# Layer norms with VectorE's order written by hand, ScalarE for the first tile's transposed copies, and a first product in the order of its operands

## The chip, the cores and the metric

The kernel runs on one core of a Trainium2 chip. The metric is the time of one execution on the device in microseconds (us), the median of several. The core's engines that matter here are TensorE (PE in the profile; its weight loads are PEld), VectorE (DVE), ScalarE (ACT), GpSimd (POOL) and SyncE (SP), which issues the transfers by DMA. Each engine works through its own list of instructions in a fixed order and waits, at an instruction, for what this instruction needs.

## What is computed

Two transformer blocks in a row, in fp32, on 256 tokens of width 1024. Block 1 has one layer: a state-space and Fourier mixer, and 32 experts of which each token uses four. Block 2 has two layers. Each has a mixer of four kinds of heads with an output projection, a layer norm over residual plus mixer, a feed-forward part (dense in the first layer, 8 experts of which two are used in the second), and another layer norm. Cut to what matters:

```python
def _layer_norm(x, g, b):
    mu = jnp.mean(x, -1, keepdims=True)
    var = jnp.mean(jnp.square(x - mu), -1, keepdims=True)
    return (x - mu) * lax.rsqrt(var + LN_EPS) * g + b

def second_block(x, ...):
    h = x.astype(F32)
    for l in range(DEPTH_2):
        p = jnp.einsum('btd,dc->btc', h, w_in[l])
        pa, pb, pc, pd = _split(p, MIXER_COLS)
        ...
        mix = jnp.einsum('btc,cd->btd', jnp.concatenate([ya, yb, yc, yd], axis=-1), w_out[l])
        h = _layer_norm(DN_ALPHA * h + mix, ln1_g[l], ln1_b[l])
        if l % 2 == 0:
            f = _swiglu(h, ffn_w_gate[i], ffn_w_up[i], ffn_w_down[i])
        else:
            f = _moe(h, moe_router[i], moe_w_gate[i], moe_w_up[i], moe_w_down[i])
        h = _layer_norm(DN_ALPHA * h + f, ln2_g[l], ln2_b[l])
    return h
```

## The kernel before

The tokens lie in two tiles of 128 partitions; `K.xres` holds the residual, [128, tile, 1024]. A phase ends with a product that TensorE accumulates in PSUM. A norm follows on VectorE, and `to_hT` transposes the normalised tiles (four 128x128 blocks to one PSUM tile, two such q per token tile) into `K.hT`, [128, 8, 256], with the features on the partitions: the operand of the next phase's products. Between `to_hT` and a product stands one more step: fp32 products are made of three products in fp32r, hi x hi, hi x lo and lo x hi (`mm3`, L340 to 344). `split` (L330) makes the two halves of weights: ScalarE copies the high half `whi` (L335), VectorE subtracts it, which is the low half `wlo` (L336). The activations are halved in the same way, one of eight blocks `kt` at a time (L1574 and L1575 in the mixers, L2204 and L2205 in the dense phase, L2165 and L2166 for the output projection, where the trace calls both halves w).

The phases of block 2 come in this order: mixer 0, norm (0,0), dense phase with 11 steps, norm (0,1), mixer 1, norm (1,0), expert phase with its router. The places between them are called seams here.

Each layer norm is done in two pieces. `layer_norm` (L1387) scales the residual and adds the product (L1403), takes the statistics (L1404, L1407), makes the reciprocal root in ten small steps (`rsqrt`, L233 to 245) and normalises (L1409). `to_hT` applies the weight and the bias of the norm to the transposed copy. The residual gets them later, in the next phase: `affine` (L1424) multiplies by a row and adds a row, each 128x1024 and for each token tile. These rows `lnr` come by DMA, spread over the partitions (`brow`, L313), and `affine_rows` issues them when the next phase runs. The residual that mixer 0 receives has one row to apply (the final norm's weight of block 1), so its affine is two instructions; that of mixer 1 is four. With `raw` (norm (1,0)) the transposed copies are made of the values before the normalisation.

The end of both mixers (L2166 to L2177) is the output projection. It goes over two halves of the features, half 1 first and half 0 last. Half 0 holds the outputs oH and oG of the two gated mixers, of which oG is last. Each half has two column halves c, whose sums for the two token tiles lie in PSUM, called pp (c = 0) and tr (c = 1), so that each (half, c) has 24 products. The rows `lnr` are queued on SyncE behind weight loads (`ahead("xb", 3)`), and the affine of the residual is written down with half 1.

The order on each engine is fixed when the kernel is built: a scheduler goes through the program by estimated times, and takes what is ready by them. `behind(K, ins)` places what stands in it after the instructions ins in that order. The order thus obtained holds on the chip, whatever the waits there are.

Of the kernel before, what the change touches and what calls it, by code (L numbers as in the profile page):

```python
# [8 lines left out]
F32 = mybir.dt.float32  # L9
BF = mybir.dt.bfloat16  # L10
I32 = mybir.dt.int32
F32R = mybir.dt.float32r
U8 = mybir.dt.uint8
AF = mybir.ActivationFunctionType
OP = mybir.AluOpType
# [209 lines left out]
def rsqrt(K, dst, src, scale, eps, iters=3):  # L225
# [10 lines left out]
    if n < 3:  # L236
        w = v
        nc.vector.tensor_scalar(w, src, -0.5 * scale, -0.5 * eps, op0=OP.mult, op1=OP.add)
        for k in range(iters):
            for c in range(n):  # L240
                c_ = slice(c, c + 1)
                nc.vector.tensor_scalar(t[:, c_], y[:, c_], w[:, c_], y[:, c_], op0=OP.mult, op1=OP.mult)
            for c in range(n):
                c_ = slice(c, c + 1)
                nc.vector.tensor_scalar((dst if k == iters - 1 else y)[:, c_], t[:, c_], 1.5, y[:, c_], op0=OP.add, op1=OP.mult)
        return
# [93 lines left out]
def mm3(K, ps, l, r, start, stop):  # L340

    K.nc.tensor.matmul(ps, lhsT=l[0], rhs=r[0], start=start, stop=False)  # L342
    K.nc.tensor.matmul(ps, lhsT=l[0], rhs=r[1], start=False, stop=False)  # L343
    K.nc.tensor.matmul(ps, lhsT=l[1], rhs=r[0], start=False, stop=stop)  # L344

# [1041 lines left out]
def layer_norm(K, A, ps, i, parts, alpha, hT, raw=False):  # L1387
# [10 lines left out]
    for tt in range(2):  # L1398
        x = h[:, tt, :]
        st = K.small.tile([128, 2, 6], F32, name="ln_s")  # L1400
        for c in range(2):
            xc = x[:, 512 * c:512 * c + 512]
            nc.vector.scalar_tensor_tensor(xc, xc, alpha, parts(tt, c), op0=OP.mult, op1=OP.add)  # L1403
            nc.vector.bn_stats(st[:, c, :], xc)  # L1404
        if raw:
            to_hT(K, ps, hT, tt, x, None)
        nc.vector.bn_aggr(mv[:, tt, :], st)  # L1407
        rsqrt(K, rs[:, tt:tt + 1], mv[:, tt, 1:2], 1.0, 1e-5)
        K.normed = nc.vector.tensor_scalar(x, x, mv[:, tt, 0:1], rs[:, tt:tt + 1], op0=OP.subtract, op1=OP.mult)  # L1409
        if not raw:  # L1410
            to_hT(K, ps, hT, tt, x, *K.lnc)
# [8 lines left out]
def affine(K, rows, tt):  # L1420

    x = K.xres[:, tt, :]
    for r_, op in zip(rows, (OP.mult, OP.add)):
        K.nc.vector.tensor_tensor(x, x, r_, op=op)  # L1424


def to_hT(K, ps, hT, tt, x, g, b=None):

    nc = K.nc
    for q in range(2):  # L1430
        pt = ps("tr", [128, 4, 128])
        transpose4(K, pt, [x[:, 128 * (4 * q + j):128 * (4 * q + j) + 128] for j in range(4)])
        if g is None:
            d = hT[:, 4 * q:4 * q + 4, 128 * tt:128 * tt + 128]
            if q:
                last = nc.scalar.activation(d, pt, AF.Copy)
            else:
                nc.vector.tensor_copy(d, pt)
            continue
        for j in range(4):  # L1440
            kt = 4 * q + j
            d = hT[:, kt, 128 * tt:128 * tt + 128]
            if b is None:
                if q:
# [3 lines left out]
            elif q:  # L1448
# [51 lines left out]
def mixers(K, A, l, nxt):  # L1500
# [71 lines left out]
    early = [split(K, w2, w0[0][:, :, 0:128], [128, 8, 128], bufs=2, after=(K.normed,))]  # L1572
    for kt in range(8):
        nc.scalar.activation(hT[0][:, kt, :], K.hT[:, kt, :], AF.Copy)  # L1574
        nc.vector.tensor_tensor(hT[1][:, kt, :], K.hT[:, kt, :], hT[0][:, kt, :], op=OP.subtract)  # L1575

    def chan(w, c0, n=128):
# [4 lines left out]
        v = early.pop(0) if early else split(K, w2, w[:, :, c0:c0 + n], [128, 8, n], bufs=2)  # L1582
# [580 lines left out]
    for half in (1, 0):  # L2163
# [3 lines left out]
        for c in range(2):  # L2167
            wo = wload(A["w2out"][l, c][:, 4 * half:4 * half + 4, :])
            v = [split(K, w2, wo[:, 2 * i:2 * i + 2, :], [128, 2, 512], bufs=2) for i in range(2)]
# [21 lines left out]
def block2_dense(K, A):  # L2191
# [10 lines left out]
    early = [split(K, w2, w[:, :, 0:128], [128, 8, 128], after=(K.normed,))]  # L2202
    for kt in range(8):
        nc.scalar.activation(hT[0][:, kt, :], K.hT[:, kt, :], AF.Copy)  # L2204
        nc.vector.tensor_tensor(hT[1][:, kt, :], K.hT[:, kt, :], hT[0][:, kt, :], op=OP.subtract)  # L2205
    acc = {}
    for n in range(11):
# [8 lines left out]
        for j in range(2):  # L2216
            pg = ps("gu", [128, 2, 256])
            for i in range(2):
                ws = early.pop() if early else split(K, w2, w[:, :, 256 * i + 128 * j:256 * i + 128 * j + 128], [128, 8, 128])
# [130 lines left out]
```

## Time and profile before

| | us |
|---|---|
| median of 3 runs | 2711.24 |
| lowest and highest run | 2710.56, 2715.84 |
| profiled execution | 2715.85 |
| its span in the profile | 2713.9 |

| engine | busy us | share of the span |
|---|---|---|
| TensorE | 2444.3 | 90% |
| VectorE | 1436.9 | 53% |
| ScalarE | 935.2 | 34% |
| GpSimd | 229.3 | 8% |

The profile gives the busy time of each engine and the releasers of waits, taken from one execution. The shares are means over stages with different limits: in the expert stage of block 1 the transfers are the limit, in the seams of block 2 a chain that goes from engine to engine. A timeline of a seam shows what stands on the chain there: a row is a group of like instructions in a run, with its start, its length, and the idle time before it and what ended that.

### The profile page before, as it was taken

How to read it: one execution, taken by the hardware profiler on the slowest of the kernel's cores; microseconds unless marked ns; L12 is line 12 of the kernel's file. 1: busy time of each engine (PE TensorE's matmuls, PEld its weight loads, DVE VectorE, ACT ScalarE, POOL GpSimd, SP SyncE). 2: the span in 40 equal slices, each digit the busy share in tenths (PEclk: the TensorE clock that was granted, in tenths of full speed). 3: DMA queues.
4: the chain of work that ended last, by engine and by line, in shares of the span. 5: the costliest groups of instructions: out<-in, count | busy, mean ns of one | idle time of the engine just before them, and what ended most of it. 6: DMA issues, size and time to landing. Idle time of an engine off the chain costs nothing. (4 is left out here: it accounts for less than half of the span.)

```text
span 2713.9 us, 47571 instructions
## 1 busy us (share of the span) xinstructions
PE 2444.3 (90%) x20018; PEld 1626.4 (60%) x20018; DVE 1436.9 (53%) x2815; ACT 935.2 (34%) x1707; POOL 229.3 (8%) x222
## 2 busy tenths in 40 slices
PE   7999999988799989998898689988998999899996
PEld 4777668864344444444344268767997876565553
DVE  5887885553343354444344466677556567412224
ACT  4444344432223222223222253373444346112121
POOL 0421432210000000000000000120000012000000
PEclk9999999999899999999999889998998999899998
DMA  6332335768899999999999942235423232788993
GB/s 266 112 126 105 123 125 188 279 223 365 344 424 425 389 426 424 425 425 424 425 425 425 371 144 83 100 118 201 179 78 121 70 125 111 296 376 359 386 423 135
DMA packets 74537, 717.13 MB, mean 264 GB/s; under 512 B 9777, under 2 KB 25656, under 8 KB 29720
## 3 DMA queue, kind: packets, MB, share of 16 engines
q1 hardware_dynamic: 74264, 713.11, 65.3%
q8 instruction: 218, 3.57, 0.5%
q14 instruction: 55, 0.45, 0.0%
HBM read 712.03 MB, written 1.05 MB: 263 GB/s over the span
## 5 line engine op out<-in xcount | busy, mean ns | idle before, releaser
L1072 PE MATMUL gu<-w,xg 128*32 128x512 f32 x4400 | 539.0, 612 | 87.9 <-PEq L1082 46.9
L336 DVE TENSOR_TENSOR wlo<-w,whi 128x1024 fp32r<-128x1024 f32 (+1 forms) x250 | 309.3, 1239 | 207.8 <-ACT whi L335 206.5
L1072 PEld LDWEIGHTS gu<-w,xg 128*32 128x32 f32 x4400 | 168.8, 111 | 409.1 <-issue 365.2
L335 ACT ACTIVATE whi<-w 128x1024 fp32r<-128x1024 f32 (+1 forms) x250 | 260.7, 1045 | 382.3 <-PE pp L343 102.1
L1145 PE MATMUL d<-w,hTk 128*32 128x256 f32 x4936 | 295.2, 385 | 17.1 <-issue 6.3
L1145 PEld LDWEIGHTS d<-w,hTk 128*32 128x32 f32 x4936 | 172.6, 111 | 114.8 <-issue 32.6
L1339 DVE TENSOR_SCALAR a<-gu 128x256 f32<-128x256 f32 x96 | 39.5, 423 | 301.5 <-PE gu L1072 239.5
L1340 ACT ACTIVATE th<-a 128x256 f32<-128x256 f32 x96 | 36.6, 413 | 392.6 <-DVE a L1339 350.7
L1163 ACT ACTIVATE hTk<-d,rc 32x256 f32<-32x256 f32 x256 | 119.7, 467 | 80.0 <-PE d L1145 48.8
L1026 PE MATMUL x<-S,h 128*128 128x192 f32 (+2 forms) x608 | 111.0, 337 | 11.7 <-DVE S L1002 5.2
L1026 PEld LDWEIGHTS x<-S,h 128*128 128x128 f32 x608 | 99.1, 197 | 28.7 <-issue 18.7
L1050 PE MATMUL x<-o,R 96*128 96x512 f32 x320 | 96.5, 443 | 18.3 <-ACT o L1170 14.8
L342 PE MATMUL pp<-big,whi 128*128 128x512 f32 (+2 forms) x296 | 110.4, 373 | 2.2 <-ACT big L474 2.2
L343 PE MATMUL pp<-big,whi 128*128 128x512 f32 (+2 forms) x296 | 110.2, 373 | 0.9 <-DVE big L475 0.5
L344 PE MATMUL pp<-big,wlo 128*128 128x512 f32 (+2 forms) x296 | 108.9, 368 | 0.0
L1123 ACT ACTIVATE hTk<-x 128x384 f32<-128x384 f32 (+1 forms) x88 | 40.5, 481 | 181.2 <-PE d L1145 113.5
L342 PE MATMUL gu<-hT,whi 128*128 128x256 f32 x352 | 100.5, 286 | 1.9 <-ACT hT L2204 1.9
L1050 PEld LDWEIGHTS x<-o,R 96*128 96x128 f32 x320 | 60.7, 205 | 66.7 <-issue 30.4
L343 PE MATMUL gu<-hT,whi 128*128 128x256 f32 x352 | 100.5, 286 | 0.0
L344 PE MATMUL gu<-hT,wlo 128*128 128x256 f32 x352 | 100.5, 285 | 0.0
L552 DVE SCALAR_TENSOR_TENSOR cacc<-pad,big,cacc 128x512 f32<-128x512 f32 (+1 forms) x128 | 97.7, 763 | 3.9 <-ACT cacc L549 1.2
L342 PE MATMUL pp<-whi,w 128*128 128x512 f32 (+1 forms) x192 | 81.9, 428 | 10.3 <-ACT w L2165 6.3
(736 smaller groups left out, 4725.7 us busy)
## 6 DMA issues: line engine op xcount, KB each, us to landing
w<-in_wgu_dram SPq DMA_DIRECT2D x155, 2048.0 KB, 20.8
w<-in_wdn_dram SPq DMA_DIRECT2D x80, 2048.0 KB, 21.9
w<-in_win_dram SPq DMA_DIRECT2D x18, 2048.0 KB, 7.7
w<-in_w2in_dram SPq DMA_DIRECT2D x30, 1024.0 KB, 5.3
w<-in_wgu2b_dram SPq DMA_DIRECT2D x16, 1536.0 KB, 10.9
w<-in_ffgu_dram SPq DMA_DIRECT2D x11, 2048.0 KB, 8.1
w<-in_wmod_dram SPq DMA_DIRECT2D x10, 2048.0 KB, 8.1
w<-in_wdn2b_dram SPq DMA_DIRECT2D x8, 1536.0 KB, 9.1
```

Of the source, the lines that this page charges most:

```text
L335: K.nc.scalar.activation(hi, src, AF.Copy)
L336: (eng or K.nc.vector).tensor_tensor(lo, src, hi, op=OP.subtract)
L342: K.nc.tensor.matmul(ps, lhsT=l[0], rhs=r[0], start=start, stop=False)
L343: K.nc.tensor.matmul(ps, lhsT=l[0], rhs=r[1], start=False, stop=False)
L344: K.nc.tensor.matmul(ps, lhsT=l[1], rhs=r[0], start=False, stop=stop)
L552: nc.vector.scalar_tensor_tensor(acc, pad[:, :S, k:k + 256], cw[:, ci, k:k + 1], acc, op0=OP.mult, op1=OP.add)
L1026: nc.tensor.matmul(px[:, j, :], lhsT=t_[:, tt, 128 * (q + j):128 * (q + j) + 128], rhs=S[:, tt, i:i + n].rearrange("p a b -> p (a b)"), st ...
L1050: nc.tensor.matmul(py, lhsT=R[:, 128 * tt:128 * tt + 128], rhs=o[i][:, 512 * c:512 * c + 512], start=i == 0, stop=i == 1)
L1072: mm = nc.tensor.matmul(p_[32 * q:32 * q + 32, :], lhsT=l_[:, kt, :], rhs=w[:, i, m * q:m * q + m], start=first, stop=True, tile_position= ...
L1123: nc.scalar.activation(aT[:, i, :, 0:c_], pt[:, :, 0:c_], AF.Copy, scale=0.5)
L1145: nc.tensor.matmul(pd[g][32 * c:32 * c + 32, :], lhsT=aT[:, pi, g, 32 * q:32 * q + 32], rhs=w[:, i, 256 * c:256 * c + 256], start=first an ...
L1163: nc.scalar.activation(dst, src, AF.Copy, scale=w_)
```

## The change

It has five parts (and `rsqrt` and `affine` now return or keep their last instruction). `layer_norm` places VectorE's statistics, aggregation, reciprocal root and normalisation one behind the other in an order written by hand, with the first tile's normalisation (and its `to_hT`) ahead of the second tile's last half of statistics; for `raw` both tiles' copies come first, and the normalisations last. `to_hT` gives ScalarE all eight copies of the first tile, of which VectorE made four. `early_split` puts the low half of the next phase's first weights behind the eight low halves of the activations. `early_product` runs that phase's first product as eight hi x hi, then eight hi x lo, then eight lo x hi. And the weights of the output projection's half 0 are split behind `K.aff`, the last affine instruction.

```diff
...
     K.nc.tensor.matmul(ps, lhsT=l[0], rhs=r[0], start=start, stop=False)
     K.nc.tensor.matmul(ps, lhsT=l[0], rhs=r[1], start=False, stop=False)
     K.nc.tensor.matmul(ps, lhsT=l[1], rhs=r[0], start=False, stop=stop)
+
+
+def early_split(K, pool, src, shape, hT, bufs):
+
+    nc = K.nc
+    hi = pool.tile(shape, F32R, name="whi", bufs=bufs)
+    lo = pool.tile(shape, F32R, name="wlo", bufs=bufs)
+    nc.scalar.activation(hi, src, AF.Copy)
+    for kt in range(8):
+        nc.scalar.activation(hT[0][:, kt, :], K.hT[:, kt, :], AF.Copy)
+        last = nc.vector.tensor_tensor(hT[1][:, kt, :], K.hT[:, kt, :], hT[0][:, kt, :], op=OP.subtract)
+    with behind(K, (last,)):
+        nc.vector.tensor_tensor(lo, src, hi, op=OP.subtract)
+    return hi, lo
+
+
+def early_product(K, ps, w, hT):
+
+    for n, (i, j) in enumerate(((0, 0), (0, 1), (1, 0))):
+        for kt in range(8):
+            K.nc.tensor.matmul(ps, lhsT=w[i][:, kt, :], rhs=hT[j][:, kt, :], start=n == 0 and kt == 0, stop=n == 2 and kt == 7)
 
 
 def row_of(K, ps, cols):
...
     K.pend = [A["lnp"][l, 2 * j:2 * j + 1], A["lnp"][l, 2 * j + 1:2 * j + 2]]
     K.lnmv = mv = K.small.tile([128, 2, 2], F32, name="ln_m")
     K.lnrs = rs = K.small.tile([128, 2], F32, name="ln_r")
-    for tt in range(2):
+    st = [K.small.tile([128, 2, 6], F32, name="ln_s") for tt in range(2)]
+    last = []
+
+    def vec(f, *args, **kw):
+        with behind(K, last[-1:]):
+            last.append(f(*args, **kw))
+
+    def stats(tt, c):
+        xc = h[:, tt, 512 * c:512 * c + 512]
+        vec(nc.vector.scalar_tensor_tensor, xc, xc, alpha, parts(tt, c), op0=OP.mult, op1=OP.add)
+        vec(nc.vector.bn_stats, st[tt][:, c, :], xc)
+
+    def normed(tt):
         x = h[:, tt, :]
-        st = K.small.tile([128, 2, 6], F32, name="ln_s")
-        for c in range(2):
-            xc = x[:, 512 * c:512 * c + 512]
-            nc.vector.scalar_tensor_tensor(xc, xc, alpha, parts(tt, c), op0=OP.mult, op1=OP.add)
-            nc.vector.bn_stats(st[:, c, :], xc)
-        if raw:
-            to_hT(K, ps, hT, tt, x, None)
-        nc.vector.bn_aggr(mv[:, tt, :], st)
-        rsqrt(K, rs[:, tt:tt + 1], mv[:, tt, 1:2], 1.0, 1e-5)
-        K.normed = nc.vector.tensor_scalar(x, x, mv[:, tt, 0:1], rs[:, tt:tt + 1], op0=OP.subtract, op1=OP.mult)
-        if not raw:
-            to_hT(K, ps, hT, tt, x, *K.lnc)
+        vec(nc.vector.bn_aggr, mv[:, tt, :], st[tt])
+        vec(rsqrt, K, rs[:, tt:tt + 1], mv[:, tt, 1:2], 1.0, 1e-5)
+        vec(nc.vector.tensor_scalar, x, x, mv[:, tt, 0:1], rs[:, tt:tt + 1], op0=OP.subtract, op1=OP.mult)
+
+    for tt, c in ((0, 0), (1, 0), (0, 1)):
+        stats(tt, c)
+    if raw:
+        to_hT(K, ps, hT, 0, h[:, 0, :], None)
+    else:
+        normed(0)
+        to_hT(K, ps, hT, 0, h[:, 0, :], *K.lnc)
+    stats(1, 1)
+    if raw:
+        to_hT(K, ps, hT, 1, h[:, 1, :], None)
+        normed(0)
+    normed(1)
+    if not raw:
+        to_hT(K, ps, hT, 1, h[:, 1, :], *K.lnc)
 
 
 def affine_rows(K, pool, tag=()):
...
 
     x = K.xres[:, tt, :]
     for r_, op in zip(rows, (OP.mult, OP.add)):
-        K.nc.vector.tensor_tensor(x, x, r_, op=op)
+        K.aff = K.nc.vector.tensor_tensor(x, x, r_, op=op)
 
 
 def to_hT(K, ps, hT, tt, x, g, b=None):
 
     nc = K.nc
+    first = tt == 0
     for q in range(2):
         pt = ps("tr", [128, 4, 128])
         transpose4(K, pt, [x[:, 128 * (4 * q + j):128 * (4 * q + j) + 128] for j in range(4)])
         if g is None:
             d = hT[:, 4 * q:4 * q + 4, 128 * tt:128 * tt + 128]
-            if q:
+            if q or first:
                 last = nc.scalar.activation(d, pt, AF.Copy)
             else:
                 nc.vector.tensor_copy(d, pt)
...
             kt = 4 * q + j
             d = hT[:, kt, 128 * tt:128 * tt + 128]
             if b is None:
-                if q:
+                if q or first:
                     last = nc.scalar.activation(d, pt[:, j, :], AF.Copy, scale=g[:, kt:kt + 1])
                 else:
                     nc.vector.tensor_scalar(d, pt[:, j, :], g[:, kt:kt + 1], None, op0=OP.mult)
-            elif q:
+            elif q or first:
                 last = nc.scalar.activation(d, pt[:, j, :], AF.Identity, scale=g[:, kt:kt + 1], bias=b[:, kt:kt + 1])
             else:
                 nc.vector.tensor_scalar(d, pt[:, j, :], g[:, kt:kt + 1], b[:, kt:kt + 1], op0=OP.mult, op1=OP.add)
...
     nc.sync.dma_start(out=g2b, in_=A["g2w"][l, 128:160])
     ws = pe_.tile([128, 8, 48], F32, name="ws")
     nc.sync.dma_start(out=ws, in_=A["w2s"][l])
-    early = [split(K, w2, w0[0][:, :, 0:128], [128, 8, 128], bufs=2, after=(K.normed,))]
-    for kt in range(8):
-        nc.scalar.activation(hT[0][:, kt, :], K.hT[:, kt, :], AF.Copy)
-        nc.vector.tensor_tensor(hT[1][:, kt, :], K.hT[:, kt, :], hT[0][:, kt, :], op=OP.subtract)
+    early = [early_split(K, w2, w0[0][:, :, 0:128], [128, 8, 128], hT, 2)]
 
     def chan(w, c0, n=128):
 
         pj = ps("pp", [n, 256])
         if isinstance(w, list):
             w, c0 = w[c0 // 256], c0 % 256
-        v = early.pop(0) if early else split(K, w2, w[:, :, c0:c0 + n], [128, 8, n], bufs=2)
+        if early:
+            early_product(K, pj, early.pop(), hT)
+            return pj
+        v = split(K, w2, w[:, :, c0:c0 + n], [128, 8, n], bufs=2)
         for kt in range(8):
             mm3(K, pj, [t_[:, kt, :] for t_ in v], [t_[:, kt, :] for t_ in hT], kt == 0, kt == 7)
         return pj
...
             nc.vector.tensor_tensor(hT[1][:, kt, :], yT[:, kt, :], hT[0][:, kt, :], op=OP.subtract)
         for c in range(2):
             wo = wload(A["w2out"][l, c][:, 4 * half:4 * half + 4, :])
-            v = [split(K, w2, wo[:, 2 * i:2 * i + 2, :], [128, 2, 512], bufs=2) for i in range(2)]
+            v = [split(K, w2, wo[:, 2 * i:2 * i + 2, :], [128, 2, 512], bufs=2, after=() if half else (K.aff,)) for i in range(2)]
             if half:
                 affine(K, lnr, c)
             for tt in range(2):
...
     ps = lambda tag, shape: pp.tile(shape, F32, name=tag, bufs=nb[tag])
     hT = [pool.tile([128, 8, 256], F32R, name=f"hT{i}") for i in range(2)]
     w = wtile(K, A["ffgu"][0])
-    early = [split(K, w2, w[:, :, 0:128], [128, 8, 128], after=(K.normed,))]
-    for kt in range(8):
-        nc.scalar.activation(hT[0][:, kt, :], K.hT[:, kt, :], AF.Copy)
-        nc.vector.tensor_tensor(hT[1][:, kt, :], K.hT[:, kt, :], hT[0][:, kt, :], op=OP.subtract)
+    early = [early_split(K, w2, w[:, :, 0:128], [128, 8, 128], hT, 3)]
     acc = {}
     for n in range(11):
         if n == 1:
...
         for j in range(2):
             pg = ps("gu", [128, 2, 256])
             for i in range(2):
-                ws = early.pop() if early else split(K, w2, w[:, :, 256 * i + 128 * j:256 * i + 128 * j + 128], [128, 8, 128])
+                if early:
+                    early_product(K, pg[:, i, :], early.pop(), hT)
+                    continue
+                ws = split(K, w2, w[:, :, 256 * i + 128 * j:256 * i + 128 * j + 128], [128, 8, 128])
                 for kt in range(8):
                     mm3(K, pg[:, i, :], [t_[:, kt, :] for t_ in ws], [t_[:, kt, :] for t_ in hT], kt == 0, kt == 7)
             th = w2.tile([128, 256], F32, name="th")
```

The end of mixer 0 on VectorE. The names: oG is the last gated output, hn_r, prow and gG its factors, wlo the low half of the projection's weights, w<-hTk,w the low half of a block of activations, lnr a row of the affine, xres the residual. Before:

```order
L336 TENSOR_TENSOR wlo<-w_16073,whi 128x1024
L250 SCALAR_TENSOR_TENSOR hn_r<-rq_t,rq_y 128x8
L2166 TENSOR_TENSOR w<-hTk,w 128x256
L1618 TENSOR_TENSOR oG<-oG,hn_r 128x512
L2166 TENSOR_TENSOR w<-hTk,w 128x256
L2081 TENSOR_TENSOR oG<-oG,prow 128x512
L2082 TENSOR_TENSOR oG<-oG,gG 128x512
L336 TENSOR_TENSOR wlo<-w,whi 128x1024
L2166 TENSOR_TENSOR w<-hTk,w 128x256 x2
L336 TENSOR_TENSOR wlo<-w,whi 128x1024
L1424 TENSOR_TENSOR xres<-xres,lnr_18009 128x1024 x2
L1403 SCALAR_TENSOR_TENSOR xres<-xres,pp 128x512
```

VectorE at the same place, now:

```order
L250 SCALAR_TENSOR_TENSOR hn_r<-rq_t,rq_y 128x8
L1658 TENSOR_TENSOR oG<-oG,hn_r 128x512
L2121 TENSOR_TENSOR oG<-oG,prow 128x512
L2122 TENSOR_TENSOR oG<-oG,gG 128x512
L2206 TENSOR_TENSOR w<-hTk,w 128x256 x4
L1463 TENSOR_TENSOR xres<-xres,lnr_18009 128x1024 x2
L336 TENSOR_TENSOR wlo<-w_16073,whi 128x1024 x2
L1424 SCALAR_TENSOR_TENSOR xres<-xres,pp 128x512
```

The low halves of the weights stand behind the affine, and no longer ahead of oG. Mixer 1 has the same order with four affine instructions.

TensorE at the end of mixer 0 now (sc<-ident,oG are the transposes of oG, pp the sums of c = 0):

```order
L1570 MATMUL sc<-ident,oH 128x128 x4
L342 MATMUL pp<-whi,w 128x512 x2
L1570 MATMUL sc<-ident,oG 128x128 x4
L343 MATMUL pp<-wlo,w 128x512
L344 MATMUL pp<-whi,w 128x512
L342 MATMUL pp<-whi,w 128x512
```

Two of half 0's 48 products stand ahead of oG's transposes, and the first that needs wlo behind them; before, products with wlo stood ahead of these transposes too.

The second norm of layer 0 on VectorE, in the middle of the two tiles' chains. Before:

```order
L1404 BN_STATS ln_s<-xres 128x6
L235 TENSOR_SCALAR rq_y<-rq_i 128x1
L238 TENSOR_SCALAR rq_v<-ln_m 128x1
L1407 BN_AGGR ln_m<-ln_s 128x2
L242 TENSOR_SCALAR rq_t<-rq_y,rq_v 128x1
L233 TENSOR_SCALAR rq_v<-ln_m 128x1
L245 TENSOR_SCALAR rq_y<-rq_t,rq_y 128x1
L234 TENSOR_SCALAR rq_i<-rq_v 128x1
```

And now, on VectorE:

```order
L245 TENSOR_SCALAR rq_y<-rq_t,rq_y 128x1
L242 TENSOR_SCALAR rq_t<-rq_y,rq_v 128x1
L245 TENSOR_SCALAR ln_r<-rq_t,rq_y 128x1
L1424 TENSOR_SCALAR xres<-xres,ln_m,ln_r 128x1024
L1424 SCALAR_TENSOR_TENSOR xres<-xres,acc 128x512
L1597 TENSOR_SCALAR prow<-prow 128x128
L1424 BN_STATS ln_s<-xres 128x6
L1601 TENSOR_SCALAR mu_20209<-mu 128x9
L1424 BN_AGGR ln_m<-ln_s 128x2
```

The small steps of the two tiles no longer stand in turn: the second tile's begin when the first tile is normalised.

## Rows read from the trace of the kernel before

**Rows 1.** Busy time of three stretches: stretch, us, PE, PEld, DVE, ACT, POOL, PEclk, DMA, GB/s

```profile
590.00:1575.00 985.00, 853.42 (x8483) 420.02 (x8482) 419.46 (x1006) 258.01 (x559) 11.78 (x14) 0.96 0.95 400
1825.00:1850.00 25.00, 15.10 (x63) 12.06 (x64) 21.36 (x57) 9.53 (x21) 0.00 (x0) 0.77 0.68 261
2300.00:2328.00 28.00, 18.23 (x90) 14.54 (x88) 24.80 (x80) 5.24 (x7) 0.30 (x1) 0.73 0.65 244
```

**Rows 2.** Timeline, block 1 to mixer 0: start us, us, engine, line, instruction

```profile
1590.33 1.56 DVE L1461 CAST posf<-posi 128x2 f32<-128x2 int32 x1
1592.43 0.32 PE L343 MATMUL pp<-w,whi 128*128 128x256 f32 x1
```

**Rows 3.** Timeline of VectorE, end of mixer 0

```profile
1818.96 1.21 DVE L336 TENSOR_TENSOR wlo<-w,whi 128x1024 fp32r<-128x1024 f32 x1
1822.16 0.69 DVE L2082 TENSOR_TENSOR oG<-oG,gG 128x512 f32<-128x512 f32 x1
1825.08 0.75 DVE L2166 TENSOR_TENSOR w<-hTk,w 128x256 fp32r<-128x256 f32 x2
1830.24 2.35 DVE L1424 TENSOR_TENSOR xres<-xres,lnr 128x1024 f32<-128x1024 f32 x2
```

**Rows 4.** Timeline of TensorE, last products of mixer 0

```profile
1832.57 0.40 PE L343 MATMUL tr<-wlo,w 128*128 128x512 f32 x1
1832.81 0.39 PE L344 MATMUL tr<-whi,w 128*128 128x512 f32 x1
```

**Rows 5.** Issue of mixer 0's row, and the transfers from 1813.6 to 1824

```profile
1813.93 0.77 SPq L313 DMA_DIRECT2D lnr<-in_fnw_dram  x1
DMA packets 410, 4.13 MB, mean 397 GB/s; under 512 B 33, under 2 KB 33, under 8 KB 34
```

**Rows 6.** Busy time in two pieces of the dense phase's first product, columns of rows 1

```profile
1848.00:1851.00 3.00, 3.00 (x16) 3.00 (x15) 3.00 (x8) 1.11 (x4) 0.00 (x0) 0.50 0.02 1
1852.00:1855.00 3.00, 3.00 (x27) 3.00 (x27) 1.59 (x3) 1.06 (x1) 0.00 (x0) 1.00 0.00 0
```

**Rows 7.** Timeline, norm (0,0) to the dense phase's first product

```profile
1840.35 1.97 PE L319 MATMUL tr<-ident,xres 128*128 128x128 f32 x8 [7.15 <-DVE xres L1409]
1841.02 0.81 DVE L1409 TENSOR_SCALAR xres<-xres,ln_m,ln_r 128x1024 f32<-128x1024 f32 x1
1847.03 0.80 PE L342 MATMUL gu<-hT,whi 128*128 128x256 f32 x2 [1.90 <-ACT hT L2204]
```

**Rows 8.** Timeline, norm (0,1) to mixer 1's first product

```profile
2045.80 0.81 DVE L1409 TENSOR_SCALAR xres<-xres,ln_m,ln_r 128x1024 f32<-128x1024 f32 x1
2051.34 2.56 ACT L1574 ACTIVATE w<-hTk 128x256 fp32r<-128x256 f32 x8
2051.82 0.79 PE L342 MATMUL pp<-w,whi 128*128 128x256 f32 x2 [1.90 <-ACT w L1574]
```

**Rows 9.** End of mixer 1: issue and landing of its rows, affine, last product

```profile
2283.39 1.29 SPq L313 DMA_DIRECT2D lnr<-in_lnp_dram  x2
DMA to landing us min/median/max: 8.9/13.5/18.1
2303.24 4.62 DVE L1424 TENSOR_TENSOR xres<-xres,lnr 128x1024 f32<-128x1024 f32 x4
2306.97 0.40 PE L344 MATMUL tr<-whi,w 128*128 128x512 f32 x1
```

**Rows 10.** Timeline of VectorE, norm (1,0) to the router

```profile
2317.03 0.27 DVE L242 TENSOR_SCALAR rq_t<-rq_y,rq_v 128x1 f32<-128x1 f32 x1
2318.21 0.81 DVE L1409 TENSOR_SCALAR xres<-xres,ln_m,ln_r 128x1024 f32<-128x1024 f32 x1
2322.78 0.35 DVE L935 SCALAR_TENSOR_TENSOR rt<-wr2r,ln_m,x 128x8 f32<-128x8 f32 x2 [1.41 <-PE x L928]
```

**Rows 11.** Timeline of VectorE, reciprocal root of block 1, two tiles in turn

```profile
1580.42 0.34 DVE L245 TENSOR_SCALAR rq_y<-rq_t,rq_y 128x1 f32<-128x1 f32 x2
1580.67 0.45 DVE L242 TENSOR_SCALAR rq_t<-rq_y,rq_v 128x1 f32<-128x1 f32 x2
```

More of the change, by code (lines that the diff above doesn't have):

```diff
@@ L244, in rsqrt @@
                 c_ = slice(c, c + 1)
-                nc.vector.tensor_scalar((dst if k == iters - 1 else y)[:, c_], t[:, c_], 1.5, y[:, c_], op0=OP.add, op1=OP.mult)
-        return
+                last = nc.vector.tensor_scalar((dst if k == iters - 1 else y)[:, c_], t[:, c_], 1.5, y[:, c_], op0=OP.add, op1=OP.mult)
+        return last
     for k in range(iters):
```

## Prediction

> **What bounds the kernel now.** I read the busy time of the stages first, then the timelines of the places where the change works. In the expert stage of block 1, 590 to 1575 us, the DMA share is 0.95 at 400 GB/s: work moved inside that stage disappears beside the weights [rows 1]. At the end of mixer 0 and around the last layer norm the DMA share is 0.68 and 0.65, VectorE is busy 21.36 of 25 us and 24.80 of 28, and TensorE has only 15.10 and 18.23 [rows 1]: there the time is a chain that goes back and forth between VectorE, ScalarE and TensorE, and each microsecond on it reaches the end. So the sum is made seam by seam. I follow the end of the last product of a phase on TensorE, called P, and the first product after the norm. What ScalarE's copies do inside the expert stage (four VectorE copies of the first tile that go to ScalarE) I cost at nothing, covered by the weights.
>
> **The change part by part.**
>
> Block 1 to mixer 0. The low half of the first weights goes behind the eight low halves of the activations. After it, on VectorE, stands the conversion of the positions, 1.56 us from 1590.33 [rows 2], and then the second product's low half. With the eight low halves done at about 1590.3 as before, that is 1590.3 + 1.2 + 1.56 + 1.2 = 1594.2 (1.21 us for one low half of weights [rows 3]), while the second product ran from 1592.43 [rows 2]: **+1.8**, between 0 (the conversion slips behind) and 3.7 (the eight low halves end later too, by about as much again, because ScalarE now has the first tile's copies ahead of the high halves that they need).
>
> End of mixer 0. This is the largest part. TensorE multiplies the last half of the output projection, and needs wlo, the low half of its weights, for one product in three. Before, VectorE made two of these low halves (1818.96 is the second) ahead of oG·gG, which ended at 1822.16 + 0.69 = 1822.85, and the affine of the residual stood last, 2.35 us from 1830.24, beside TensorE's products, where it cost nothing [rows 3]. Now those two low halves stand behind the affine, and the affine needs a row that comes by DMA. Step by step. Without the two low halves (2 x 1.21) and two low halves of activations (0.75) oG·gG ends 3.1 earlier, near 1819.7. From there to the last low halves of the activations it took 2.98 before (TensorE's transposes, ScalarE's copy and high halves, and VectorE's low halves until 1825.08 + 0.75 = 1825.83 [rows 3]), so VectorE is free for the affine at 1822.7. The row was issued at 1813.93 behind three weight loads of together 4.2 MB; until 1824 the queues had moved 4.13 MB at 397 GB/s [rows 5]. With the row's 0.5 MB, 4.7 MB at that rate from 1813.6 end at 1825.4. The affine then runs until 1827.75, the first wlo until 1829.0. TensorE has done 2 of its 48 products by then and waits; 46 x 0.24 = 11.0 (0.24 from start to start [rows 4]) end at 1840.0. TensorE has then been idle for most of 8 us, and the granted clock after such a pause is the next term: after the wait before the first product at 1847.03 the clock read 0.50 until 1851, with 16 products in 3 us, and 1.00 from 1852, with 27 [rows 6, 7]. Five microseconds at the lower level lose 5 x 11/27 = 2.0. So P is 1842.0 in place of 1832.81 + 0.39 = 1833.2 [rows 4]: **+8.8**. If the row is there in time and the clock stays, it is 1822.7 + 2.35 + 1.21 + 11.0 = 1837.3, +4.1; the upper end is +10.
>
> First norm of block 2 and the dense phase's first product. Before, the transposes began 7.15 after P and the first product at 1847.03, P + 13.8 [rows 7]. Now the first tile's half that is ready while TensorE is still at the second is finished first, and its transposes can begin 4 us earlier; but the second tile's chain starts behind it, the steps of the two reciprocal roots stand alone, and two more affine operations, 2.3 [rows 3], have been placed inside the second chain. The second tile is normalised at about P + 9 to 9.5 (before, 1841.02 + 0.81 = P + 8.6 [rows 7]), and the first product starts near P + 12, at the pace of ScalarE's high halves, then needs the low ones: it ends where it ended. **0**, from -1 to +2.
>
> Dense phase to mixer 1. Here nothing is hidden: both tiles' sums come at one time. A reciprocal root has ten small steps per tile. Where a chain runs alone, four of them take 2318.21 - 2317.03 = 1.18, or 0.29 each [rows 10]; where two tiles' steps stand in turn, two take 1580.67 - 1580.42 = 0.25, or 0.125 each [rows 11]. One chain after the other is 20 x 0.29 = 5.8; before, it was 20 x 0.125 and, by estimate, 1.0 more for the steps at the end that stood alone already, 3.5. So +2.3 on the second tile. Against it the path from the second tile's normalisation (2045.80) to the first product (2051.82), which leads over VectorE's copies and ScalarE's high halves [rows 8], shortens by 1.2, as VectorE no longer has a low half of weights between its copies. The product itself, paced by eight high halves of 2.56/8 = 0.32 [rows 8], is 0.8 longer. Sum **+1.7**, from 0.5 to 2.5.
>
> End of mixer 1. As mixer 0, with two rows and so four affine operations, 4.62 us from 2303.24, of which two follow the last row. The rows were issued at 2283.39, and the slower of them took 18.1 to land: 2301.5 [rows 9]. Two additions, 2.3, end at 2303.8, wlo at 2305.0, 46 products at 2316.0, with the clock's 2.0 at 2318.0. Before, P was 2306.97 + 0.40 = 2307.4 [rows 9]: **+10.6**. The lower end is that of mixer 0 and the two further operations, 4.1 + 2.3 = 6.4; the upper 11.
>
> Last norm to the router. From P to the router's result it took 2322.78 - 2307.4 = 15.4 [rows 9, 10]. The transposes of both tiles no longer stand behind VectorE's copy and the chains; the raw values go to TensorE first, and the normalisation (2318.21) is off the path to the router's product. I take **-2.3**, between -5 and -1.
>
> The sum: 1.8 + 8.8 + 0 + 1.7 + 10.6 - 2.3 = +20.6. The profiled run took 2715.85 (2713.9 and 2 around it), so 2736.4 in it; it lay 4.6 above the median of 2711.24, and by the median the forecast is 2731.8, say 2732. All low ends together give +5, all high ends +28.
>
> On the interleaved steps a rule bears that speaks against my +2.3. By the rows, steps of two chains in turn start 0.125 apart and those of one chain alone 0.29 [rows 10, 11]. The Trainium skill, "VectorE: DVE Perf Modes", section "The DRAIN you can't avoid", says that the next operation doesn't start until the pipe has emptied, and that a semaphore between costs nothing extra; by that, two chains in turn would take as long as one after the other, and un-interleaving would be free. The rows speak against it, but they are few: it is rival D.
>
> **The rivals.** B: the rows land in time and the clock stays up, so that both mixers cost only their lower ends: 1.8 + 4.1 + 0 + 1.7 + 6.4 - 2.3 = +11.7, **2723**. For it: the row's landing in mixer 0 isn't shown, only bounded. Against: 18.1 us is measured for mixer 1.
>
> D: un-interleaving is free at both norms where I charged it: 2.3 less in each, **2727**.
>
> C, the faster side: TensorE doesn't wait for wlo behind the affine. It decides whether its wait there is under about 2 us at both mixers. Then the shorter pauses keep the clock up in the first products: 24 products at 27 in 3 us, not 16, is 4.5 - 2.7 = 1.8 less, three times 5.4 [rows 6]; with -2.3 and +1.7 it is -6, **2705**. Against: VectorE's order has the affine ahead of wlo without a choice, and 2.35 and 4.62 us alone [rows 3, 9] exceed that point.
>
> E: the change doesn't do what it says: waits elsewhere (the weights' DMA) already set the seams, and what moves is hidden: **2711**. Against: DMA share 0.65 to 0.68 there [rows 1].
>
> **How the numbers follow.** Forecast 0.62, B 0.16, D 0.10, C 0.06, E 0.06. 0.2%, what a measurement of this kernel tells from no change, is 5.4 us. Faster by more: 0.06 (C). Within: 0.06 (E). Slower: 0.88. The range takes in B and D and the upper ends, 2717 to 2740; C, E and a tail are left out.
>
> **What would show it.** In the changed kernel's trace: at the ends of both mixers TensorE idle before a product pp<-wlo, released by VectorE, some 8 us long, the affine just ahead of wlo on VectorE and itself waiting for a DMA; P 9 and 11 us later against the work before it; a granted clock of 0.50 after the wait. At the first norm of block 2 the transposes of the first tile 3 to 5 us earlier after P, the first product's end unchanged. At the second, the second tile's normalisation 2 us later. At the last, the router's result 2 us earlier after P. The prediction is wrong if the row is long in the memory when VectorE reaches the affine, or if low halves of VectorE were ahead of need by more than the affine takes.

## The result and the profile after

The changed kernel took 2731.01 us (median of 4 runs, 2727.52 to 2734.28) where the kernel before took 2712.85 beside it: a ratio of 1.0063, with a 95% interval from 1.0049 to 1.0077. Measured again beside the kernel before on one chip, it was 2731.00 and a ratio of 1.0070 (1.0053 to 1.0087). So the change costs 17 to 19 us. The prediction was 2732, with a range from 2717 to 2740. The size is right; what follows shows that the two large terms were right in their cause, and that the small ones came out near in part from other causes than the sum gave.

The end of mixer 0 in the changed kernel, timeline (start us, us, engine, line, instruction, and in brackets the idle time ahead of it and what ended it); the answer to [rows 3], [rows 4] and [rows 5]:

```profile
1816.51 0.69 SPq L313 DMA_DIRECT2D lnr<-in_fnw_dram  x1
1822.30 0.69 DVE L2122 TENSOR_TENSOR oG<-oG,gG 128x512 f32<-128x512 f32 x1
1824.82 0.76 DVE L2206 TENSOR_TENSOR w<-hTk,w 128x256 fp32r<-128x256 f32 x2 [1.16 <-ACT w L2205]
1829.33 2.36 DVE L1463 TENSOR_TENSOR xres<-xres,lnr 128x1024 f32<-128x1024 f32 x2 [3.75 <-DMA lnr<-in_fnw_dram]
1831.61 2.35 DVE L336 TENSOR_TENSOR wlo<-w,whi 128x1024 fp32r<-128x1024 f32 x2
1822.32 0.72 PE L342 MATMUL pp<-whi,w 128*128 128x512 f32 x2 [1.27 <-ACT w L2205]
1832.88 0.79 PE L343 MATMUL pp<-wlo,w 128*128 128x512 f32 x1 [9.18 <-DVE wlo L336]
1846.83 0.39 PE L344 MATMUL tr<-whi,w 128*128 128x512 f32 x1
```

Read it as a chain: the row is issued at 1816.51 and lands 12.8 us later. VectorE has nothing to do for 3.75 us, does the affine, then wlo, and TensorE, which has done two products and the transposes, has been idle for 9.18 us. The granted clock behind this wait, in the columns of [rows 1]:

```profile
1833.00:1836.00 3.00, 3.00 (x7) 2.36 (x8) 0.96 (x1) 0.00 (x0) 0.00 (x0) 0.50 0.02 5
1839.00:1842.00 3.00, 2.48 (x11) 1.60 (x10) 1.85 (x3) 2.21 (x3) 0.00 (x0) 1.00 0.01 3
```

It is at the lower of the two levels (1.2 of 2.4 GHz) after the pause. Mixer 1 is the same with four affine instructions, the answer to [rows 9]:

```profile
2298.68 1.31 SPq L313 DMA_DIRECT2D lnr<-in_lnp_dram  x2
2315.49 4.63 DVE L1463 TENSOR_TENSOR xres<-xres,lnr 128x1024 f32<-128x1024 f32 x4 [2.23 <-DMA lnr<-in_lnp_dram]
2320.03 2.35 DVE L336 TENSOR_TENSOR wlo<-w,whi 128x1024 fp32r<-128x1024 f32 x2
2321.31 0.79 PE L343 MATMUL pp<-wlo,w 128*128 128x512 f32 x1 [9.31 <-DVE wlo L336]
2335.10 0.39 PE L344 MATMUL tr<-whi,w 128*128 128x512 f32 x1
```

And the places of [rows 2], [rows 7], [rows 8] and [rows 10], in their order:

```profile
1594.72 0.39 PE L344 MATMUL pp<-w,wlo 128*128 128x256 f32 x1 [1.04 <-DVE wlo L336]
1850.02 1.25 PE L319 MATMUL tr<-ident,xres 128*128 128x128 f32 x8 [2.81 <-DVE xres L1424]
1856.97 1.94 PE L319 MATMUL tr<-ident,xres 128*128 128x128 f32 x8 [5.69 <-DVE xres L1424]
1859.05 0.91 PE L365 MATMUL gu<-hT,whi 128*128 128x256 f32 x2
2062.01 0.81 DVE L1424 TENSOR_SCALAR xres<-xres,ln_m,ln_r 128x1024 f32<-128x1024 f32 x1
2347.35 0.35 DVE L956 SCALAR_TENSOR_TENSOR rt<-wr2r,ln_m,x 128x8 f32<-128x8 f32 x2
```

For the rest of this text the span is cut into ten stretches at marks that every kernel has: the last step of block 1 (nr_ssq), the first result of mixer 0 (rkvT), the product oH·gH, P, the dense phase's first activation (th), its P, mixer 1's result wa, oH·gH, P, the router's result rt, the end. Each number is the difference of two starts in the timeline (P is a last product's start plus its length). "Before" is three profiles of that kernel (the first and two more), "after" two.

| stretch, us | before | after | difference of means |
|---|---|---|---|
| block 1's end to mixer 0's first result | 16.7, 17.0, 16.6 | 17.4, 17.4 | +0.7 |
| to oH·gH of mixer 0 | 222.3, 220.9, 222.2 | 223.5, 223.5 | +1.7 |
| to P of mixer 0 | 16.1, 16.2, 16.2 | 27.6, 27.2 | +11.2 |
| to the dense phase's first activation | 23.0, 23.1, 23.0 | 22.8, 22.7 | -0.3 |
| to its P | 183.0, 183.0, 183.0 | 182.6, 182.5 | -0.4 |
| to wa of mixer 1 | 36.3, 36.5, 36.4 | 37.5, 37.4 | +1.1 |
| to oH·gH of mixer 1 | 214.2, 214.2, 214.1 | 216.1, 213.9 | +0.8 |
| to P of mixer 1 | 17.6, 17.6, 17.6 | 29.3, 28.5 | +11.2 |
| to the router's result | 15.4, 15.4, 15.4 | 11.9, 11.9 | -3.6 |
| to the end | 391.1, 387.9, 387.5 | 385.0, 386.3 | -3.2 |

With block 1 (1578.3 and 1579.0) that is +19.9. The seams, in which the change works, come back within some tenths, so a single profile tells a part of 1 us there. Block 1, the long middles of the mixers and the last stretch scatter by up to 4 us from one profile of a kernel to the next, and all times with them: the kernel before ran from 2704.1 to 2717.4 in 49 runs beside the first eight experiments.

### The profile page after: what moved, and what is told of

Read it like the earlier page. It is cut to its first block, busy times and chain, and to the rows that moved or that the text cites. A ratio compares the mean times of both kernels' runs of the same rounds, so it can differ in the third digit from the quotient of the medians.

```text
span 2732.3 us, 47588 instructions
## 1 busy us (share of the span) xinstructions
PE 2446.8 (90%) x20018; PEld 1632.3 (60%) x20018; DVE 1437.8 (53%) x2801; ACT 939.5 (34%) x1721; POOL 231.1 (8%) x222
## 5 line engine op out<-in xcount | busy, mean ns | idle before, releaser
L343 PE MATMUL gu<-hT,whi 128*128 128x256 f32 x344 | 97.4, 283 | 0.0
L342 PE MATMUL gu<-hT,whi 128*128 128x256 f32 x344 | 97.4, 283 | 0.0
L343 PE MATMUL pp<-wlo,w 128*128 128x512 f32 (+1 forms) x192 | 79.0, 412 | 19.6 <-DVE wlo L336 19.6
## 6 DMA issues: line engine op xcount, KB each, us to landing
w<-in_wgu2b_dram SPq DMA_DIRECT2D x16, 1536.0 KB, 11.5
```

## The experiments

In what follows "the gate" is the part of the change that puts the split of half 0's weights behind the affine.

**The gate undone.**

```diff
-            v = [split(K, w2, wo[:, 2 * i:2 * i + 2, :], [128, 2, 512], bufs=2, after=() if half else (K.aff,)) for i in range(2)]
+            v = [split(K, w2, wo[:, 2 * i:2 * i + 2, :], [128, 2, 512], bufs=2) for i in range(2)]
```

> The changed kernel with one part undone: the weights of the output projection's half 0 are split without waiting in the order for the affine. Theory (TensorE waits for wlo behind the affine, 11.4 us at the end of mixer 0 and 11.6 at mixer 1 by the changed kernel's trace): both go, 2731 - 23 = 2708, and what is left is the sum of the other parts, 2.0 - 0.2 + 1.2 - 3.6 = -0.6 against the kernel before, so 2707 to 2714. In its trace no wait of TensorE over 2 us before pp<-wlo. Rival (the norm's hand order and the first products cost the time): it stays above 2720.

Measured: 2716.90 beside 2710.64, ratio 1.0017 (1.0005 to 1.0028), or +1.4 to +7.6. P of mixer 0 is back at 16.16 and of mixer 1 at 18.0, and TensorE's longest wait at the end of mixer 0 is the one ahead of the first product, 1.27:

```profile
1821.02 0.50 PE L342 MATMUL pp<-whi,w 128*128 128x512 f32 x1 [1.27 <-ACT w L2205]
1825.24 0.72 PE L342 MATMUL tr<-whi,w 128*128 128x512 f32 x2 [0.39 <-ACT whi L335]
```

So both long waits are the gate's, and the rival falls; but some 6 us are left, and not the -0.6 that I expected: from P to the first activation it is now 26.75 and not 22.8, and to the router 16.1 and not 11.9. The gate had been paying something back there.

**The gate alone**, in the kernel before (the same line with its `after`, and `K.aff` kept in `affine`).

> The kernel before with that one part alone: the split of half 0 behind the affine. Theory: +23 against the kernel before, 2731 to 2738, with waits of 8 to 10 us of TensorE before pp<-wlo at the end of both mixers and a granted clock of 0.50 for about 5 us behind each. Rival: under +10, if the wait needs the other parts.

Measured: 2724.35, ratio 1.0053 (1.0035 to 1.0072), +9.5 to +19.5, less than expected. The waits are there, 9.26 and 10.89:

```profile
1827.27 0.80 PE L343 MATMUL pp<-wlo,w 128*128 128x512 f32 x1 [9.26 <-DVE wlo L336]
2309.77 0.80 PE L343 MATMUL pp<-wlo,w 128*128 128x512 f32 x1 [10.89 <-DVE wlo L336]
```

The granted clock is 0.50 behind the first wait and 1.00 again from 1832. Both stretches to P are longer, by 11.0 (27.15) and 11.9 (29.5). But the stretches behind are shorter, by 3.4 (19.6 to the first activation) and 4.9 (10.5 to the router). The sum is +14.5, the measured ratio +14.4. What VectorE's rows show there: the affine is no longer the last thing ahead of the norm, so VectorE takes the sums of pp while TensorE is still at tr (the first at 1832.14, with P at 1841.1); before, the first stood behind the affine, at 1832.5 with P at 1833.2. That this is the reason for the shorter stretches is tested below, with the affine in VectorE's slot: for the larger part of them it is.

```profile
1823.72 2.36 DVE L1424 TENSOR_TENSOR xres<-xres,lnr 128x1024 f32<-128x1024 f32 x2 [3.83 <-DMA lnr<-in_fnw_dram]
1832.14 0.69 DVE L1403 SCALAR_TENSOR_TENSOR xres<-xres,pp 128x512 f32<-128x512 f32 x1 [3.79 <-PE pp L344]
```

**The hand order of the norm alone**, in the kernel before (the new `layer_norm`; `K.normed` is its last normalisation).

```diff
+    for tt, c in ((0, 0), (1, 0), (0, 1)):
+        stats(tt, c)
...
+    normed(1)
+    K.normed = last[-1]
```

> The kernel before with the hand order of the layer norm alone (copies, first split and first product as before). Theory: norm (0,1) has the second tile normalised 2.3 us later after the last product (11.6 in place of 9.4), and the first product as much later, less what it gets back from the copies; norm (1,0) has the router's result 2 to 3.5 earlier; norm (0,0) nothing. Together -1.5 to +2, so not to be told from the kernel before. Rival (un-interleaving is free, since the next operation starts only when the pipe is empty): the second tile at norm (0,1) is normalised within 0.5 of before, and the sum is -2 to -4.

Measured: 2720.43, ratio 1.0040 (1.0027 to 1.0053), +7.3 to +14.4. My expectation was wrong here by more than its range. The stretches: +4.5 from P to the first activation (27.5), +2.6 to wa (39.0), and +1.2 to the router, where I had expected a gain; together +8.3. At norm (0,1) the second tile's last statistics begin when the first is normalised, the first tile's four copies on VectorE come in between, and the second tile's steps are 0.56 apart for two:

```profile
2045.90 0.81 DVE L1403 TENSOR_SCALAR xres<-xres,ln_m,ln_r 128x1024 f32<-128x1024 f32 x1
2047.96 1.35 DVE L1470 TENSOR_SCALAR hTk<-tr,ln_c,ln_c 128x128 f32<-128x128 f32 x4
2050.09 0.27 DVE L242 TENSOR_SCALAR rq_t<-rq_y,rq_v 128x1 f32<-128x1 f32 x1
2050.65 0.28 DVE L242 TENSOR_SCALAR rq_t<-rq_y,rq_v 128x1 f32<-128x1 f32 x1
2051.76 0.81 DVE L1403 TENSOR_SCALAR xres<-xres,ln_m,ln_r 128x1024 f32<-128x1024 f32 x1
```

The second tile is normalised from 2051.76, 10.5 us after that kernel's P (2041.23), where it was from 2045.80, 6.6 after P (2039.20), before [rows 8]. Of these 3.9 the four copies are 1.3 (the next operation starts at 2049.23). With the copies on ScalarE, in the changed kernel and with the gate undone, the second tile is normalised from 9.4 after P, 2.8 later than before. So putting one tile's chain behind the other's is not free: the rival that has it free falls. My 2.3 had left out the copies.

**The affine behind the second normalisation**, on top of the hand order.

```diff
-            affine(K, lnr, n // 2 - 1)
+            with behind(K, (K.normed,)):
+                affine(K, lnr, n // 2 - 1)
```

> The kernel before with the hand order of the norm, and the next phase's affine placed behind the second normalisation. With the hand order alone the dense phase's first result came 4.5 later after the last product. Theory: 2.4 of it are the two affine operations inside the second tile's chain, the rest the chains one behind the other: now 2.1 to 2.3 later. Rival: the affine fills gaps that VectorE has between the chain's steps, and 4.5 stays.

Measured (one profile): 26.4 from P to the first activation, where the hand order alone has 27.5 and the kernel before 23.0. The second tile is normalised 2.0 us earlier than with the hand order alone (11.8 after P, not 13.8), as the two affine operations of 1.2 us would have it, but only 1.2 of it reaches the dense phase. So of the 4.5 at this norm 1.2 is the affine's place and 3.4 the rest of the hand order. Neither of the two numbers I had given is right.

**The first split and first product alone**, in the kernel before (`early_split` and `early_product`, and their two places of use).

> The kernel before with the first split and the first product in the new order alone (low half of the first weights last; hi x hi, hi x lo, lo x hi). Theory: block 1 to mixer 0 +2.0 (the conversion of the positions stands ahead of the second product's low half); at norms (0,0) and (0,1) the transposed copies no longer wait behind a low half of weights, -1.2 each, and the product gets 0.8 longer: together +1 to +2, 2712 to 2716. Rival (the new order of operands lets the first product begin so much earlier that it pays): -2 or better, 2711 or less.

Measured: 2716.78, ratio 1.0018 (1.0005 to 1.0032), +1.4 to +8.7. In its profile the seams have +0.6 at mixer 0's first result (17.4), +0.2 at the first activation (23.2) and nothing at wa (36.4) and at the router (15.4). So this part costs about 1 us where it works, and the rival falls. The median, 6.1 above the kernel before, is higher than that and just outside what I expected; the profile has its surplus in block 1 and in the last stretch (392.3), which scatter, so what the rest is stays open.

**The rows first**, in the changed kernel.

```diff
-    ahead("xb", 3)
+    xb = rpool(K.bst, "xb", 3)
     lnr = affine_rows(K, rpool(st, "xln"))
+    for _ in range(3):
+        K.slots.append((xb, "w"))
+        K.ahead.append(wtile(K, nxt[len(K.ahead)], xb.tile([128, 4096], F32, name="w")))
```

> The changed kernel with the affine's rows issued ahead of the three weight loads, and nothing else. Theory (affine waits for the row behind weight loads): VectorE's idle time of 3.75 and 2.23 us before the affine, put down to the DMA, goes; TensorE's wait before pp<-wlo is 5.4 and 7.1 in place of 9.2 and 9.3; the time falls by 5.9 to 2725, and does not reach the kernel before, since the affine's own 2.35 and 4.63 stay ahead of wlo. Rival (the row's own landing time or its queue's place later on sets it): the idle time stays and the time is 2731. Second rival (the row is all of it): 2715 or less.

Measured: 2722.60, ratio 1.0046 (1.0029 to 1.0063), +7.9 to +17.1. That is 8.4 below the changed kernel, where the theory had 5.9, and the way is another. The row, issued ahead of the three loads, is there 4.2 us later, and not 12.8:

```profile
1812.00 0.33 SPq L313 DMA_DIRECT2D lnr<-in_fnw_dram  x1
1816.24 1.23 DVE L1463 TENSOR_TENSOR xres<-xres,lnr 128x1024 f32<-128x1024 f32 x1 [0.42 <-DMA lnr<-in_fnw_dram]
1818.07 1.22 DVE L1463 TENSOR_TENSOR xres<-xres,lnr 128x1024 f32<-128x1024 f32 x1
```

But the scheduler has now put the two operations into the middle of oH's chain. So oH·gH comes 2.6 later than in the changed kernel (226.1 from mixer 0's first result), and P 8.6 to 9.0 earlier behind it (18.5; 20.3 in mixer 1). TensorE's waits of 5.4 and 7.1 for wlo did not come: none is over 1.0. So the run confirms that loads ahead of the row are what it waits for, and does not measure the affine alone ahead of wlo.

**The affine in VectorE's slot**, a version that the runs above point to: the kernel before with the rows first, the multiplications behind the last low halves of the activations and ahead of the last wlo, additions (mixer 1) behind it, and the norm's sums behind these.

```diff
+        if not half:
+            aff(0, OP.mult, last)
...
+            v = [split(K, w2, wo[:, 2 * i:2 * i + 2, :], [128, 2, 512], bufs=2, after_lo=(K.aff,) if c and i and not half else ()) for i in range(2)]
...
+    if l:
+        aff(1, OP.add, K.lo)
+    K.first = (K.lo, K.aff)
```

> The kernel before with rows first, and the affine (its multiplications) in the slot in which VectorE waited 3.26 and 2.29 us for the last high half of the weights, ahead of the last wlo alone; in mixer 1 the additions stay behind it. Theory (what the gate gave back at the norms, 3.4 and 4.9, comes from the affine being off the product's end, so that the sums of pp are taken while TensorE is at tr): norm (0,0) 2.5 to 3.5 shorter, norm (1,0) 2 to 3 shorter, no wait of TensorE for wlo over 1 us: 4.5 to 6.5 faster than the kernel before. Rival (the gate gave back by the later start of TensorE alone): within 2 of the kernel before.

Measured: 2709.62 beside 2710.95, ratio 0.9994 (0.9983 to 1.0005), no difference that can be told, where I expected 4.5 to 6.5; by the time alone the rival holds. The seams do what the theory says, though less at the first: P of both mixers unmoved (16.15, 17.63), the first activation 1.9 earlier (21.1), the router 3.2 earlier (12.3). So of the 3.4 and 4.9 that the gate gave back, 1.9 and 3.2 come without its stall, by the affine's place; what the rest is, and why the time does not show these gains, stays open. VectorE's rows at mixer 0, before and then in this run:

```profile
1829.09 1.22 DVE L336 TENSOR_TENSOR wlo<-w,whi 128x1024 fp32r<-128x1024 f32 x1 [3.26 <-ACT whi L335]
1822.09 2.35 DVE L2172 TENSOR_TENSOR xres<-xres,lnr 128x1024 f32<-128x1024 f32 x2
1825.43 1.23 DVE L337 TENSOR_TENSOR wlo<-w,whi 128x1024 fp32r<-128x1024 f32 x1 [0.99 <-ACT whi L335]
1826.57 1.28 DVE L1405 SCALAR_TENSOR_TENSOR xres<-xres,pp 128x512 f32<-128x512 f32 x2
```

The affine stands in the wait of 3.26 that VectorE had for the high half, of which 0.99 is left, and P does not move.

**The slot and the copies**: the same with the first tile's copies on ScalarE, as in the change.

```diff
+    first = tt == 0
...
-            if q:
+            if q or first:
```

> The kernel before as in the run with the affine in VectorE's slot, and with the first tile's copies on ScalarE as in the change. Theory: the copies are worth 1.0, 1.5 and 0.5 at the norms (the difference of the changed kernel without the gate and its two other parts, stretch by stretch), so 3 less than with the slot alone, 7 to 10 faster than the kernel before. Rival (those differences are the parts' interplay and the copies are worth nothing by themselves): as with the slot alone.

Measured: 2708.38, ratio 0.9988 (0.9980 to 0.9997), 0.8 to 5.4 us faster than the kernel before, and so the only version that is clear of it on the fast side. Its seams are 2.3, 0.9 and 4.9 shorter (20.8 to the first activation, 35.5 to wa, 10.5 to the router), 8.0 together; that is the expected size, but in the time it is less than the 7 to 10 that I expected. Against the slot alone the copies are worth 0.4, 0.5 and 1.7 at the norms, not 1.0, 1.5 and 0.5. In its profile the middle of mixer 0 was 224.7 and thus 2.9 longer, which the kernel before does not show in three profiles, and the last stretch 390.6, with a low clock of its own (last section). Whether these come back was not measured, so why the rest is not in the time stays open.

**Both kernels again.** The expectations were these:

> The kernel before, profiled again, to see how far single stretches scatter. The seams (from the end of a phase's last product to the next phase's first results) within 0.3 us of the first profile, block 1's end within 3. The last stretch, router's result to the end, took 391.1 in the first profile and 385.0 in that of the changed kernel: if its 6 us are scatter, it is now between 385 and 392 without a rule; if a later router gives them back, it is 391 again.

> The kernel before, a third profile. From the router's result to the end 391.1 and 387.9 in the first two, 385.0 in the changed kernel. If it is scatter, anything from 385 to 392; stretches at the seams within 0.3.

> The changed kernel again, beside the kernel before on one chip. The stretches of the first profile that the change touches come back within 0.5 us: +11.4 and +11.6 at the ends of the mixers, -0.2, +1.2 and -3.6 behind the norms, +0.8 at the first product. Those that it doesn't touch, +1.3 and +1.9 inside the mixers and -6.1 from the router to the end, are scatter by one theory and come out otherwise; by the other they belong to the change (a clock that another course of waits has set) and come back too. Time +13 to +21 against the kernel before.

The table above has what came out. The seams are within 0.4 in the kernel before and 0.8 in the changed one, so they belong to the kernels; the ends of the mixers came back as +11.0 and +10.8, the second outside the 0.5 that I had given. The +1.9 in the middle of mixer 1 did not come back (216.1, then 213.9), but the changed kernel with the gate undone and with the rows first has it too (216.1 and 216.0): it comes and goes, and why is open. The +1.3 in mixer 0's middle did come back (223.5 twice, and 223.4 with the gate undone). The last stretch is partly scatter: the first profile of the kernel before has 391.1 and a stretch of low clock from 2480 (rows in the last section); its two other profiles have no such dip, and 387.9 and 387.5. What is left of the difference, about 2, stays open.

## Why the prediction was right

**The ends of the mixers** (forecast +8.8 and +10.6, measured +11.2 and +11.2). Right in the cause: with the gate undone both go, with the gate alone they are there. In the first three sizes were short. The row landed at 1829.33 - 1816.51 = 12.8 after its issue, and not 11.5: +1.3 (the sum had taken one mean rate for all that is queued). The lower clock held from 1832.88 to 1838.5, with products 0.43 apart where 0.235 is usual, and cost 2.6, not 2.0. And the second column half had its own short wait for wlo, worth 0.7, which the sum had not. Together 2.6, the excess of that profile (11.4). In mixer 1 three things came otherwise. The rows were there 2.5 earlier beside oH·gH than the sum had it: their issue stood 7.6 ahead of oH·gH and not 6.3 as before, and the first landed after 16.8, not 18.1. (The 18.1 of [rows 9] is the second row's alone, and counts from its own issue at 2284.15, so that it landed at 2302.3 and not 2301.5.) But then all four affine operations followed, 4.63, and not two: the second row landed at 2316.7, 1.2 behind the first, so the multiplications had waited too. And the lower clock with the second column half's wait cost 3.2, not 2.0. That +10.6 came out near +11.2 (11.6 and 10.8 in the two profiles) is thus partly luck.

**The norms** (forecast 0, +1.7 and -2.3; measured -0.3, +1.1 and -3.6). At norm (0,0) what the sum lists is in the trace: the transposes begin 2.8 after P and not 7.15, the second tile is normalised at P + 9.6, the first product starts at P + 11.8. But I had put this down to the hand order, and it is the gate's work. With the gate undone the three are 6.8, 13.5 and 15.7; the hand order alone costs 4.5 there, and the gate gives back 3.4 to 3.9 (26.75 without it and 22.8 with it), for the larger part because the affine leaves the end of the product. At norm (1,0) I had put the gain down to the raw values going to TensorE first; the hand order alone loses 1.2 there, and the gate gives back 4.3 to 4.9. So the step that failed at both, though the numbers came near, is to take the stall only as a loss at the product's end: the affine, which had stood last ahead of the norm, moved into the stall, and the norm's first sums ran beside the products that followed.

At norm (0,1) the second tile is normalised from 9.4 after P in place of 6.6, +2.8 against the +2.3 of the sum. From there to the first product it is 4.80 in place of 6.02, which is the -1.2 of the sum, but not by its reason: with the low half's new place alone it is 6.02, and with the hand order alone, where the low half still stands ahead of those of the activations, 4.74. The product, which should get 0.8 longer, has its first 24 in 4.9 in place of 5.3. The three terms of the sum also add up to 1.9, where it says 1.7.

All in all the ends of the mixers came out 3.0 above the forecast and the norms 2.2 below it; that these nearly cancel in the total is luck.

**Block 1 to mixer 0** (forecast +1.8): +0.7 at the first result and 1.0 more at the second, where the wait of 1.04 for the second product's wlo stands in the row at 1594.72. As worked out. With the first split and product alone the second result is as late, but mixer 0's middle has its old length (222.0), so that this 1.0 reaches the end is not shown.

**The rivals.** B needed the row in time; it was 3.75 late. D (un-interleaving is free): refuted by 6.6 against 9.4 at norm (0,1). The time alone would not do it, since D's 2727 lies within the interval of the ratio (2726 to 2734). There the rule of the Trainium skill in "VectorE: DVE Perf Modes", section "The DRAIN you can't avoid", that a next operation waits until the pipe is empty, read by itself, does not fit these short steps: in turn they start 0.125 apart [rows 11], though each lasts some 0.2 to 0.27, and in one chain 0.28. The same section adds that an operation that isn't held starts earlier, and with that the trace agrees. C needed a wait under 2 us; it was 9.2 and 9.3. E (what moves is hidden) had 2711, where 2731 was measured.

## What to carry to other kernels

An instruction that waits for a DMA takes everything behind it on its engine into the wait; before an order puts it ahead of something that another engine needs, look where its transfer stands in the queue (4.2 us issued first, 12.8 behind three loads). A stall is not a plain loss: here the gate cost 11.0 and 11.9 at the products and gave back 3.4 and 4.9 behind them, so the stretch behind a wait is to be read with the wait. Two short dependent chains on one engine are faster in turn than one behind the other (2.8 us for a norm's two tiles). Work that fits a known gap of an engine can be put into that gap by name: the seams got 1.9 and 3.2 shorter, though the time did not show it until the copies were added.

## What the runs showed of the hardware

Where a program's long stretches have not changed, they still scatter: the last stretch from 385.0 to 392.3 in thirteen profiles of these kernels. The two longest, 391.1 and 392.3, have a low granted clock some 160 us behind the router's result that the others don't have there, and the third, 390.6 (the slot and the copies), has one some 45 us behind it that is its own. In the first profile of the kernel before, TensorE was busy for 2.60 of 5 us from 2475, and then had a clock of 0.50 (stretch, us, PE, PEld, DVE, ACT, POOL, PEclk, DMA share, GB/s):

```profile
2475.00:2480.00 5.00, 2.60 (x59) 1.97 (x48) 0.00 (x0) 0.00 (x0) 0.00 (x0) 1.00 0.99 419
2480.00:2485.00 5.00, 5.00 (x29) 3.03 (x28) 3.77 (x10) 0.89 (x3) 0.00 (x0) 0.50 1.02 436
```

So a pause of 2.4 us in all, while the DMA share was 0.99, was followed by the lower level there. In the two other profiles of this kernel TensorE was busy for 2.47 of the 2.5 us at the place of the longest pause, and the clock stayed at 1.00. That one such pause with its dip goes with an end 3 us later, as much as some of the parts are worth, I had not expected.
